# A decoder layer's expert values read in the order of a list made on the chip, with a branch around the unused ones

## The chip, the cores and the metric

The kernel runs on one core of one Trainium2 chip. The metric is the device time of one execution in microseconds. Three executions of the kernel before took 1772.38, 1773.74 and 1774.95 us; their median, 1773.74, is the time before. The profile is of one more execution, taken by the hardware profiler.

The core's engines, by the names in the profile: PE (TensorE's matmuls) and PEld (its weight loads, which overlap them), DVE (VectorE), ACT (ScalarE), POOL (GpSimd) and SP (SyncE, which here only issues transfers). Sixteen DMA engines move the data. POOL issues transfers through the queue q0, SP through q1.

## The reference

One decoder layer for 256 tokens of width 2048, float32: attention in two groups of heads, a feed-forward part called PEER, and a gated embedding, each closed by a layer norm. The change lies in PEER and in what stands around it. PEER keeps 16,384 experts, each one row of u and one row of v (2048 numbers). A token picks 16 experts in each of 8 heads, by product keys: an expert's number is 128 × ia + ib, with ia and ib out of 128 keys each.

```python
def peer_ffn(x, wq, sub_keys, u, v):
    ...
    va, ia = lax.top_k(sa, PEER_TOPK)
    vb, ib = lax.top_k(sb, PEER_TOPK)
    cand = (va[..., :, None] + vb[..., None, :]).reshape(t, PEER_HEADS, PEER_TOPK * PEER_TOPK)
    cidx = (ia[..., :, None] * PEER_NKEYS + ib[..., None, :]).reshape(t, PEER_HEADS, PEER_TOPK * PEER_TOPK)
    top, sel = lax.top_k(cand, PEER_TOPK)
    eidx = jnp.take_along_axis(cidx, sel, axis=-1)
    gates = jax.nn.softmax(top, axis=-1)
    ...
        ub = u[eb]
        vbk = v[eb]
        act = jax.nn.gelu(jnp.einsum('thed,td->the', ub, xb).astype(jnp.float32))
        w = (gb * act).astype(xb.dtype)
        return jnp.einsum('the,thed->td', w, vbk)
```

So a token's result is the sum over its 128 picks of gate × gelu(u row · x) × v row.

## The kernel before

PEER is computed in two ways at once. The first 100 of the 256 tokens (NSP) are *gathered*: for each, POOL fetches the 128 u rows that it picked by one indirect transfer of 1 MB (L890, into one of four buffers gb), VectorE takes the dot products (L857), and later the same with the v rows, which VectorE scales and accumulates (L867). The other 156 tokens (NDT) are *dense*: TensorE multiplies them with all of u and all of v, and weights that are zero where an expert wasn't picked make the sum right. GROUPS ((0,64), (64,32), (96,4)) says how the gathered tokens are laid out: in a group of n tokens, each one's 128 picks are spread over 128/n columns of partitions.

The stages, in the order of TensorE's work:

1. Attention, output projection, first layer norm, and the query projection with top-k (L206 ps_q among them). Gathers begin here.
2. u, dense: 128 blocks of 128 experts (one block for each ia; u_block, L999 to L1002). Each is one load of 1 MB by SP (wf<-peer_u) and 16 float32 matmuls of 128 × 128 by 156 columns (L206 in gemm_T32), each of which the profile shows as two instructions. ScalarE's gelu writes the block's 128 × 156 result to its place in A0 (6 blocks), A1 (up to block SEG1 = 64) or A2 (the rest); W_of gives the place.
3. Beside u's second part runs gate_work (L934 to L989) for the first 64 rows of ia, and beside v's first 64 steps for the rest. In groups of GB = 5 tokens, VectorE writes one-hot matrices of each token's picked ia (eq, L949) and ib (ohb, L951), ScalarE scales eq by the gates' high and low halves (hi, lo, L955, L956), TensorE multiplies ohb with both (L963, L964: two float16 matmuls a token and part), which gives the gate of every expert for that token, and VectorE multiplies A with it (scale, L973). OHB = 5 sets of buffers let the one-hot matrices be made ahead of the matmuls.
4. v, dense, in two passes over all 128 blocks, one for each half of the 2048 columns: v_load takes a pair of half blocks per 1 MB load by SP (wf<-peer_v), and v_mm (L1069) adds 8 matmuls of 156 columns per half block into 4 PSUM banks. v_banks (L1076) opens the banks with matmuls of zeros, v_out adds a bank into the residual XF.
5. Tail: the last STAG = 6 blocks of v are held back and multiplied column by column, so that transposes of finished columns (res1, res2), the sums of the first two gathered groups over their partitions (natural_parts, natural_out, L902 to L919) and of the third (third_sums, L921) stand between them. Then the gated embedding and the last layer norm.

What sets the order: a scheduler orders each engine's instructions when the kernel is built, and each engine then takes them in that order; instructions given to keep stay in the order of the program. Gathers are paced twice: gathers(rate) hands out so many per block (GQ 1.8 per head in the queries, GU 0.60 and GUG 0.75 per u block, GVG 0.42 and GV 0.35 per half block of v), and before each gather POOL copies a 4-byte mark that SP loads (L886 to L888), so that a gather can't run ahead of SP's loads.

## Time and profile before

| | us |
|---|---|
| median of three executions | 1773.74 (1772.38 to 1774.95) |
| the profiled execution | 1771.9 |
| its span, first to last instruction | 1770.1 |
| PE busy | 1758.6 |
| DVE busy | 1058.2 |
| ACT busy | 541.7 |
| POOL busy | 527.4 |

A row of a group reads: line, engine, operation, output<-inputs by the program's names, shapes, xcount, then busy us and mean ns of one instruction, then the engine's idle time just before them and what ended it. A matmul row gives the shape of its moving operand: 128x156 is 128 rows by 156 columns; the mean of a matmul includes the time in which the next one already runs, so the time per instruction in a dense stretch is shorter than it. A row of the chain of waits gives start, length and what it is; a row of a window gives its limits and length, then for each engine busy time and instructions, the granted clock of TensorE (1.00 is full), the busy share of the DMA engines and GB/s.

### The profile page before, as it was taken

What the parts mean: (1) busy time and instruction counts of PE and PEld (TensorE: products, weight loads), DVE (VectorE), ACT (ScalarE), POOL (GpSimd) and SP (SyncE); (2) the same over time, 40 slices, a digit from 0 to 9 for tenths busy, and PEclk for the clock granted to TensorE, in tenths of its full rate; (3) what the DMA queues carried; (4) which work ended last, traced back from release to release, by engine and by line L of the source; (5) the groups of instructions that cost most, each with busy time, mean ns of one, the idle gap of its engine ahead of it and who ended that gap; (6) DMA issues with size and microseconds to landing.
All of it is one profiled execution on the core that took longest, in us unless ns stands there. A gap on an engine that the chain in (4) does not pass through costs nothing.

```text
span 1770.1 us, 30377 instructions
## 1 busy us (share of the span) xinstructions
PE 1758.6 (99%) x12092; PEld 1650.8 (93%) x12092; DVE 1058.2 (60%) x1698; ACT 541.7 (31%) x1350; POOL 527.4 (30%) x556
## 2 busy tenths in 40 slices
PE   9999999999999999999999999999999999999998
PEld 7888888878889999999999999999999999999887
DVE  5565589664699877355655645886343433344686
ACT  5677468732110100104333324561000000000452
POOL 0133033105346227332333233323333323322000
PEclk9999999999999999999999999999999999999999
DMA  7554644566998999999999999999999999999671
GB/s 288 190 166 165 231 152 155 179 259 227 383 418 309 421 417 415 421 420 420 419 421 411 421 420 419 414 419 399 421 420 420 421 421 417 420 420 404 228 267 61
DMA packets 99823, 606.23 MB, mean 342 GB/s; under 512 B 12824, under 2 KB 14416, under 8 KB 35776
## 3 DMA queue, kind: packets, MB, share of 16 engines
q1 hardware_dynamic: 67792, 388.04, 55.3%
q0 software_dynamic: 30160, 213.10, 29.3%
q10 hardware_dynamic: 1728, 3.15, 0.5%
q8 instruction: 95, 1.56, 0.4%
q14 instruction: 48, 0.39, 0.1%
HBM read 598.36 MB, written 6.03 MB: 341 GB/s over the span
## 4 chain that ended last, share of the span: by engine, by line
PE 95%; DMA 3%; DVE 1%; issue 1%; ACT 0%; POOL 0%; POOLq 0%; ACTq 0%; SPq 0%; DVEq 0%
PE ps_v L1069 31%; PE ps_u L206 29%; PE ps_qk L194 7%; PE ps_q L206 6%; PE ps_qk L196 4%; DMA wf<-peer_u 2%; PE ps_v L213 2%; PE ps_v L215 2%; PE ps_v L214 2%; PE ps_gate L213 1%; PE ps_gate L215 1%; PE ps_gate L214 1%; PE ps_mix L214 1%; PE ps_mix L215 1%; PE ps_mix L213 1%
## 5 line engine op out<-in xcount | busy, mean ns | idle before, releaser
L1069 PE MATMUL ps_v<-A,wf 128*128 128x156 f32 x4096 | 552.4, 297 | 0.0
L1069 PEld LDWEIGHTS ps_v<-A,wf 128*128 128x128 f32 x4096 | 544.9, 190 | 0.8
L206 PE MATMUL ps_u<-XF,wf 128*128 128x156 f32 x3904 | 528.9, 297 | 1.5 <-DMA wf<-peer_u 1.2
L206 PEld LDWEIGHTS ps_u<-XF,wf 128*128 128x128 f32 x3904 | 519.2, 190 | 3.1 <-issue 1.6
L867 DVE SCALAR_TENSOR_TENSOR y<-gb,ew,y 128x2048 f32<-128x2048 f32 x94 | 220.8, 2349 | 219.1 <-DMA gb<-v_rows,eig 214.5
L857 DVE SCALAR_TENSOR_TENSOR gb<-gb,xq 128x2048 f32<-128x2048 f32 x100 | 231.7, 2322 | 146.0 <-DMA gb<-u_rows,eig 146.0
L888 POOL COPY pace<-mark 1x1 f32<-1x1 f32 x200 | 122.3, 612 | 528.6 <-DMA mark<-c_iota 527.4
L116 DVE TENSOR_TENSOR wl<-wf,wh 128x1024 fp32r<-128x1024 f32 (+1 forms) x199 | 212.7, 1091 | 103.5 <-ACT wh L115 101.6
L115 ACT CAST wh<-wf 128x1024 fp32r<-128x1024 f32 (+1 forms) x199 | 172.1, 892 | 141.8 <-PE ps_v L215 34.0
L194 PE MATMUL ps_qk<-X,wh 128*128 128x512 f32 x512 | 185.2, 401 | 0.0
L1002 ACT ACTIVATE A<-ps_u 128x156 f32<-128x156 f32 x128 | 38.4, 300 | 433.4 <-PE ps_u L206 338.2
L890 POOL DMA_INDIRECT gb<-u_rows,eig x100 | 126.6, 1266 | 125.6 <-DVE gb L857 67.6
L890 POOL DMA_INDIRECT gb<-v_rows,eig x100 | 130.0, 1300 | 65.7 <-DVE y L867 28.8
L196 PE MATMUL ps_qk<-X,wl 128*128 128x256 f32 x512 | 145.7, 285 | 0.0
L955 ACT ACTIVATE hi<-eq,ghf 128x64 f16<-128x64 f16 x312 | 104.5, 335 | 45.2 <-DVE eq L949 41.9
L194 PEld LDWEIGHTS ps_qk<-X,wh 128*128 128x128 f32 x512 | 96.4, 188 | 21.9 <-issue 1.0
L206 PE MATMUL ps_q<-XF,wf 128*128 128x256 f32 x512 | 113.6, 379 | 0.6 <-DVE XF L535 0.6
L1130 ACT COPY x<-ps_y 128x256 f32<-128x256 f32 (+3 forms) x12 | 5.2, 439 | 345.9 <-DVE st L1129 345.7
L206 PEld LDWEIGHTS ps_q<-XF,wf 128*128 128x128 f32 x512 | 95.9, 190 | 13.1 <-DVE XF L535 0.8
L956 ACT ACTIVATE lo<-eq,glf 128x64 f16<-128x64 f16 x312 | 104.2, 334 | 0.0
L196 PEld LDWEIGHTS ps_qk<-X,wl 128*128 128x128 f32 x512 | 96.3, 188 | 2.5 <-issue 1.3
L973 DVE SCALAR_TENSOR_TENSOR A<-ps_G,A 128x30 f32<-128x30 f32 (+2 forms) x96 | 32.6, 369 | 47.2 <-PE ps_G L964 34.4
(273 smaller groups left out, 1807.3 us busy)
## 6 DMA issues: line engine op xcount, KB each, us to landing
wf<-peer_v SPq DMA_DIRECT2D x128, 1024.0 KB
wf<-peer_u SPq DMA_DIRECT2D x122, 1024.0 KB
wf<-w_qk SPq DMA_DIRECT2D x64, 512.0 KB
wf<-w_out SPq DMA_DIRECT2D x32, 512.0 KB
wf<-peer_wq SPq DMA_DIRECT2D x16, 1024.0 KB
wf<-ple_gate SPq DMA_DIRECT2D x16, 1024.0 KB
wf<-w_v SPq DMA_DIRECT2D x16, 512.0 KB
wf<-w_sv SPq DMA_DIRECT2D x15, 512.0 KB
```

The lines of the kernel that those rows point to most:

```text
L115: self.order(nc.scalar.copy(wh, src))
L116: self.order(nc.vector.tensor_tensor(wl, src, wh.bitcast(F32), op=ALU.subtract))
L194: nc.tensor.matmul(ps, wh[:, j * P:(j + 1) * P], xt[:, dt, :], start=dt == 0, stop=False)
L196: nc.tensor.matmul(ps[:, :T], wl[:, j * P:(j + 1) * P], xt[:, dt, :T], start=False, stop=dt == ND - 1)
L206: nc.tensor.matmul(ps[:, :T - t0], wf[:, dt * P:(dt + 1) * P], xt[:, dt, t0:], start=dt == 0, stop=dt == ND - 1)
L857: keep(nc.vector.scalar_tensor_tensor(g, g, 1.0, xq[i], op0=ALU.mult, op1=ALU.mult, accum_out=eact[i][:, j:j + 1]))
L867: keep(nc.vector.scalar_tensor_tensor(ys[i], g, ew[i][:, j:j + 1], ys[i], op0=ALU.mult, op1=ALU.add))
L888: keep(nc.gpsimd.tensor_copy(pace, mark))
L890: keep(nc.gpsimd.indirect_dma_start(out=g, out_offset=None, in_=a[kind], in_offset=bass.IndirectOffsetOnAxis(ap=eig[i][:, 0, j:j + 1], axi ...
L955: nc.scalar.mul(hi[:, j, :], eq[:, j, :], ghf[:, t])
L956: nc.scalar.mul(lo[:, j, :], eq[:, j, :], glf[:, t])
L1069: return nc.tensor.matmul(ps[:, (j % 2) * NDT:(j % 2 + 1) * NDT], vf[:, j * P:(j + 1) * P], W_of(ia), start=False, stop=ia == NIA - 1 and ...
```

## The change

- 88 tokens are gathered, in groups of 64, 16 and 8, and 168 are dense. The last two groups are both summed by third_sums.
- gate_work runs in two parts of 68 and 60 rows of ia (SEG1 = 68), in groups of 3 tokens with 4 sets of buffers. A third matmul per token and part (ohb by eq) accumulates over all dense tokens how often each expert was picked (cnt).
- Behind each part's gates list_work makes a list. It stores the part's weights A to memory (s_w0, s_w1; 17 stores by SP in 8-row cuts), turns cnt into a mask, gives every expert a position, used ones first and the others behind them, and inverts that: for each of the 68 or 60 rows, three VectorE comparisons (row, and both planes of blk) and one matmul put each expert's number at its position. The results are idxV (rows of v) and idxW (rows of s_w).
- v runs once over all 2048 columns, in 6 PSUM banks, in blocks of 128 listed experts: v_fetch reads 128 rows of v (1 MB) and their 168 weights (86 KB) by two indirect transfers on POOL, up to LEAD = 4 blocks ahead, in 5 buffers. 46 blocks of part 0 and 40 of part 1 (CAPS) always run; the other 42 stand in a branch that is taken if the list of either part is longer than its cap (total, read into a register).
- Marks are off in v, paces are new, STAG is 3, and the sums of group 0 stand within v's second part.

```diff
-SEG1 = 64
+SEG1 = 68
-GROUPS = ((0, 64), (64, 32), (96, 4))
+PARTS = ((0, SEG1), (SEG1, SEG2))
+CAPS = (46, 40)
+GROUPS = ((0, 64), (64, 16), (80, 8))
-GU, GUG = 0.60, 0.75
-GV, GVG = 0.35, 0.42
+GU, GUG, GUL = 0.80, 0.80, 0.5
+GV, GVG = 0.7, 0.65
-GB = 5
+GB = 3
+LISTED = 6
-EARLY, HEARLY = 6, 7
-OHB = 5
-STAG = 6
+EARLY, HEARLY = 5, 7
+OHB = 4
+STAG, LEAD, NWC = 3, 4, 8
...
+                nc.tensor.matmul(cnt[:, :ns], ohb[:, j, :], eq[:, j, :], start=t0 + j == NSP,
+                                 stop=t0 + j == T - 1)
...
+        yield from list_work(oh, parts, s0, ns, cnt)
+
+    def list_work(oh, parts, s0, ns, cnt):
...
+                cuts.append((a[f"s_w{part}"][:, a0:a0 + n], At[:, c:c + n]))
...
+        keep(nc.vector.tensor_scalar(m, cnt[:, :ns], 1.0, None, op0=ALU.min))
...
+        keep(nc.tensor.matmul(ps[:ns, :P], m, ones16, start=True, stop=True))
...
+        keep(nc.tensor.matmul(ps[:, ns:ns + 1], cols[:ns], ones16[:ns, :1], start=True, stop=True))
+        keep(nc.tensor.matmul(ps[:, :ns], ahead, m, start=True, stop=False))
+        keep(nc.tensor.matmul(ps[:, :ns], cols[:ns], ahead[:ns, :ns], start=False, stop=True))
...
+        keep(nc.vector.tensor_scalar(ov, used[:, ns:ns + 1], -float(CAPS[part] * P), 0.0,
+                                     op0=ALU.add, op1=ALU.max))
...
+        for ia in range(ns):
+            row = oh.tile([P, P], F16, name="row", tag="row", bufs=2)
+            blk = oh.tile([P, 2, SEG1], F16, name="blk", tag="blk", bufs=2)
+            keep(nc.vector.tensor_scalar(row, io128, rank[:, ia:ia + 1], None, op0=ALU.is_equal))
+            keep(nc.vector.tensor_scalar(blk[:, 0, :ns], io128[:, :ns], pos[:, ia:ia + 1],
+                                         lin[:, 0:1], op0=ALU.is_equal, op1=ALU.mult))
+            keep(nc.vector.tensor_scalar(blk[:, 1, :ns], io128[:, :ns], pos[:, ia:ia + 1],
+                                         float(ia), op0=ALU.is_equal, op1=ALU.mult))
+            keep(nc.tensor.matmul(
+                ps[:, :2 * SEG1].rearrange("p (i b) -> p i b", i=2)[:, :, :ns],
+                row, blk[:, :, :ns], start=ia == 0, stop=ia == ns - 1))
+            if ia % LISTED == LISTED - 1:
+                store(1)
+                yield
...
+        keep(nc.vector.scalar_tensor_tensor(iw, ib, float(ns), pia, op0=ALU.mult, op1=ALU.add))
+        keep(nc.vector.tensor_scalar(ib, ib, float(s0 * NKEY), None, op0=ALU.add))
+        keep(nc.vector.scalar_tensor_tensor(iv, pia, float(NKEY), ib, op0=ALU.mult, op1=ALU.add))
...
+    def v_fetch(i, b, vpool, wpool, tags):
+        vf = vpool.tile([P, D], F32, name="vf", tag=tags[0], bufs=WF if vpool is sup else 2)
+        wc = wpool.tile([P, NDT], F32, name="wc", tag=tags[1], bufs=NWC if vpool is sup else 2)
+        for dst, src, idx in ((wc, a[f"s_w{i}"].rearrange("p a t -> (p a) t"), idxW[i]),
+                              (vf, a["v_rows"], idxV[i])):
+            keep(nc.gpsimd.indirect_dma_start(
+                out=dst, out_offset=None, in_=src,
+                in_offset=bass.IndirectOffsetOnAxis(ap=idx[:, b:b + 1], axis=0)))
+        return vf, wc
...
+        if ia >= NIA - 4:
+            fetched.append(v_fetch(*order.pop(0), sup, wcp, ("wf", "wc")))
+        gathers(GUG if made < 38 else GUL)
...
+    def v_blocks(n, wpool):
+        for _ in range(n):
+            while order and len(fetched) <= LEAD and (not order[0][0] or len(idxV) > 1):
+                fetched.append(v_fetch(*order.pop(0), sup, wpool, ("wf", "wc")))
+            block = fetched.pop(0)
+            for d in range(ND):
+                v_mm(d, *block, False)
...
+    for b in range(CAPS[0]):
+        if b == CAPS[0] - LEAD:
             while not done:
                 done = run(work, 1)
-        v_block(0, ia, psv)
+        v_blocks(1, wcp)
         if not done:
-            done = run(work, 1 + (ia % 8 == 7))
-        gathers(GVG if ia < SEG1 else GV)
+            done = run(work, 4 if b < 27 else 1)
+        gathers(GVG if b < 27 else GV)
+    keep(nc.vector.tensor_tensor(total, over[0], over[1], op=ALU.add))
+    more = nc.values_load(total[0:1, 0:1], min_val=0, max_val=NIA * NKEY)
+    with tc.If(more > 0):
+        for i, b in rest:
+            block = v_fetch(i, b, fbp, fbp, ("vf", "wc_"))
+            for d in range(ND):
+                v_mm(d, *block, False)
+    pools.close("fbp", "ohp", "a2p")
+    wcq = pools.open("wcq", "left", bufs=1)
+    for _ in range(LEAD + 1):
+        v_blocks(1, wcq)
         gathers(GV)
```

Lines of the changed kernel that the prediction names: L1069, L1070 and L1072 are the three comparisons of a list step, L1074 its matmul, L1083 to L1087 the last operations that make idxV and idxW, and the count and the branch follow at L1241 to L1243.

More of the change, by code (lines that the diff above doesn't have):

```diff
@@ L1038, in build @@
             A1 = a1p.tile([P, SEG1 - SEG0, NDT], F32, name="A1")
-            iaT, ibT = (a1p.tile([P, T], F16, name=nm) for nm in ("iaT", "ibT"))
-            ghf, glf = (a1p.tile([P, T], F32, name=nm) for nm in ("ghf", "glf"))
         u_block(ia, W_of(ia))
         run(work, 1)
-        gathers(GU)
+        gathers(GU if ia >= EARLY else 1.5)
     while not run(work, 1):
```

295 lines of the change are left out of this document (179 added, 116 removed).

## The prediction

> **What bounds the kernel now.** I read the profile's page first, then the two largest groups.
>
> ```profile
> PE 1758.6 (99%) x12092; PEld 1650.8 (93%) x12092; DVE 1058.2 (60%) x1698; ACT 541.7 (31%) x1350; POOL 527.4 (30%) x556
> ...
> DMA packets 99823, 606.23 MB, mean 342 GB/s; under 512 B 12824, under 2 KB 14416, under 8 KB 35776
> ...
> q1 hardware_dynamic: 67792, 388.04, 55.3%
> q0 software_dynamic: 30160, 213.10, 29.3%
> ...
> PE 95%; DMA 3%; DVE 1%; issue 1%; ACT 0%; POOL 0%; POOLq 0%; ACTq 0%; SPq 0%; DVEq 0%
> ...
> L1069 PE MATMUL ps_v<-A,wf 128*128 128x156 f32 x4096 | 552.4, 297 | 0.0
> ...
> L206 PE MATMUL ps_u<-XF,wf 128*128 128x156 f32 x3904 | 528.9, 297 | 1.5 <-DMA wf<-peer_u 1.2
> ```
>
> TensorE is busy for 99% of the span and makes 95% of the chain that ended last; nothing else is near. So a matmul removed is worth its time, and a new wait of TensorE costs its full length, since there is no idle time that could swallow it. DMA moves 342 GB/s on the mean, two thirds of it from SP's queue (q1), one third from POOL's (q0).
>
> Next the chain of waits, for what a matmul costs where TensorE never stops, and the windows of two such stretches (columns: the stretch, its length, busy time and instructions of PE, PEld, DVE, ACT, POOL, then clock, DMA share and GB/s; the third row is the first stretch again, of L206 alone).
>
> ```profile
> 514.61 6.91 PE ps_q L206 x32
> 521.96 6.91 PE ps_q L206 x32
> ...
> 1234.03 298.92 PE ps_v L1069 x2256
> ```
>
> ```profile
> 803.33:1052.87 249.54, 249.54 (x2095) 248.16 (x2095) 140.57 (x207) 88.59 (x364) 80.54 (x86) 1.00 1.01 419
> 1234.03:1532.95 298.92, 298.92 (x2258) 298.92 (x2258) 111.08 (x51) 0.00 (x0) 96.52 (x100) 1.00 1.01 420
> ```
>
> ```profile
> 803.33:1052.87 249.54, 246.42 (x1793) 238.93 (x1793) 1.00 1.01 419
> ```
>
> One v instruction of 156 columns takes 298.92/2256 = 132.5 ns. A float32 matmul is two of them, a block of 16 matmuls 4.24 us. In the first stretch 2095 − 1793 = 302 gate matmuls (L963, L964) stand among u instructions and take what those leave: (249.54 − 1793 × 0.1325)/302 = 39.6 ns each. In pure v the DMA engines are full at 420 GB/s, and yet TensorE is busy throughout: the loads run ahead there.
>
> **What TensorE gains.** All against the profiled execution, whose span is 1770.1 us.
>
> Columns 156 → 168: by proportion 142.7 ns. The two 256-column rows of the chain give 6.91/32 = 216 ns within a piece, so (216 − 132.5)/100 × 12 = 10.0 ns more, 142.5; by their starts, 7.35/32 = 230 ns, 144.2. I take 142.7 (16 matmuls: 4.57 us) and keep 144.2 as the upper end, +10 us over 6848 instructions. Then:
> - u: 128 blocks of 32 instructions, 4096 × 10.2 ns = +41.8.
> - v: 4096 × 132.5 ns = 542.7 go, 86 × 32 = 2752 at 142.7 = 392.7 come: −150.0.
> - gates: 168 tokens × 2 parts × 3 matmuls = 1008 in place of 624; 384 more at 39.6 ns = +15.2. The upper end is the busy time of the row below, 27.6 us/312 = 88 ns: +33.8.
> - the list's 128 matmuls (136 columns or fewer, float16) lie between a gate's 40 ns and a float32 half of 132 ns; nearer the gate, 60 ns: +8 (5 to 17).
> - the sums of the last groups double their 32 small matmuls, +3.7; the sums of group 0 lose 8 of 512 columns, 185.2 us/512 = 0.36 each, −2.9. Together +0.8.
>
> ```profile
> L963 PE MATMUL ps_G<-hi,ohb 128*128 128x64 f16 x312 | 27.6, 193 | 0.0
> L924 PE MATMUL ps_y<-sel,gb 128*128 128x32 f32 x32 | 3.7, 271 | 0.0
> ...
> L194 PE MATMUL ps_qk<-X,wh 128*128 128x512 f32 x512 | 185.2, 401 | 0.0
> ```
>
> Sum: 41.8 − 150.0 + 15.2 + 8 + 0.8 = **−84.2 us** of TensorE's own work.
>
> **What the list costs.** The branch's blocks are skipped only if the list shows 46 × 128 or fewer used experts in part 0 and 40 × 128 in part 1. From the inputs that the reference draws I count, over the 168 dense tokens, 5870 of 5888 and 5084 of 5120: it is not taken.
>
> The list itself is work that nothing here has done before: per row of keys three VectorE comparisons (L1069, L1070, L1072 of the changed kernel) into double buffers (row, blk), then one matmul (L1074). In the order in which the changed kernel issues its instructions most of these matmuls are spread 2 to 4 to a block, behind which VectorE's step hides. But three runs have nothing between them: 10 in part 0 some ten u blocks before v, the last 28 of part 0 with three u blocks left, and the last 36 of part 1 straight behind block 45 of v. There TensorE goes at VectorE's pace, and behind each list matmul the u or v blocks wait.
>
> One step, by the nearest rows:
>
> ```profile
> L442 DVE TENSOR_SCALAR sm<-sm,rz,nlam 128x128 f32<-128x128 f32 x8 | 3.6, 456 | 0.3
> L703 DVE TENSOR_SCALAR CJ<-CI 128x16 uint32<-128x16 uint32 x8 | 1.3, 166 | 0.1
> L703 DVE TENSOR_SCALAR CJ<-CI 128x128 uint32<-128x128 uint32 x1 | 0.2, 220 | 0.0
> ...
> L429 DVE SCALAR_TENSOR_TENSOR sm<-ps_s,dmask 128x256 f32<-128x256 f32 x16 | 6.4, 415 | 0.9 <-PE ps_s L426 0.9
> L443 DVE SCALAR_TENSOR_TENSOR sm<-sm,rz 128x256 f32<-128x256 f32 x8 | 3.8, 478 | 0.1
> ...
> L867 DVE SCALAR_TENSOR_TENSOR y<-gb,ew,y 128x2048 f32<-128x2048 f32 x94 | 220.8, 2349 | 219.1 <-DMA gb<-v_rows,eig 214.5 <-issue 4.4
> ```
>
> Without a pointer operand 16 columns take 166 ns and 128 take 220, 0.48 ns a column; a pointer adds 478 − 415 = 63 ns. So L1069 (128 columns, one pointer) is 283 ns, L1070 (68, two) 317, L1072 (68, one) 254: 0.854 us. These elements are half as wide; with half of the column term it is 0.79. I take **0.80 us**. Lower end: no pointer cost, 0.54. Upper end: the two-pointer row of 128 columns itself, 456 ns for L1070, 0.99.
>
> A run of n steps stalls TensorE for n × 0.80, plus VectorE's gather accumulations among them (2.35 us each, L867), less n × 0.06 of own work and the two steps done ahead. Ten with one accumulation: 8.0 + 2.35 − 0.6 − 1.6 = 8.2. Twenty-eight with two: 22.4 + 4.7 − 1.7 − 1.6 = 23.8. Thirty-six with none: 28.8 − 2.2 − 1.6 = 25.0. Together **57.0 us** (at 0.54: 39.3; at 0.99: 69.9).
>
> **What the end of the list costs.** Behind the last list matmul TensorE must read a register with the count and branch. VectorE first makes the indices (L1083 to L1087, four small operations, 0.8 us), then takes three accumulations that stand ahead of the count, 7.05, then the count itself, 0.2. For the register read and the branch no row exists: at least one small instruction's 0.17 us, at most the 22.5 us that a transfer is under way when the engines are full (rows below: issued 1303.37, used 1325.90, the fourth buffer on). I take 3, near the low end, because a register is four bytes and TensorE's feed pauses just then. 0.8 + 7.05 + 0.2 + 3 = **11.1 us**. Block 46's own fetch waits for the same indices: 0.8, two POOL issues of 1.3 and one 1 MB load at 420 GB/s, 2.5, about 6 to 8 us, inside the 11.
>
> ```profile
> 1303.37 0.96 POOL L890 DMA_INDIRECT gb<-v_rows,eig  x1 [0.16 <-DVE y L867]
> ```
>
> ```profile
> 1325.90 2.35 DVE L867 SCALAR_TENSOR_TENSOR y<-gb,ew,y 128x2048 f32<-128x2048 f32 x1 [5.44 <-DMA gb<-v_rows,eig]
> ```
>
> ```profile
> L890 POOL DMA_INDIRECT gb<-v_rows,eig x100 | 130.0, 1300 | 65.7 <-DVE y L867 28.8 <-issue 25.6 <-DVE eq L949 4.1
> ```
>
> **What moves between queues.** All of v now comes through POOL: two indirect transfers a block (wc 128 × 672 B, vf 1 MB), ahead of 0.65 to 0.7 gathers. In the pure part a block needs 1.049 + 0.086 + 0.65 × 1.049 = 1.816 MB in 4.57 us, 397 GB/s; the windows show 420 with both queues. POOL's own time is 2.65 × 1.3 = 3.4 of 4.57 us. So it fits, with 5% to spare. Not taking the branch makes POOL wait for its outstanding transfers, but blocks 46 to 49 are among these, 18 us of TensorE's work. I put down 4 us for the feed (0 to 37, below).
>
> SP gains 17 stores of A to memory (11 MB) that stand ahead of u loads; four blocks are loaded ahead, 18 us, and the u stage needs 413 GB/s at most (1.8 × 1.049 MB in 4.57 us): nothing, or up to the 14 us that 5.8 MB take at 420 if that lead is gone; the stall of the list then covers it. POOL loses its waits for marks in v:
>
> ```profile
> POOL pace L888 <- DMA mark<-c_iota: 527.4, 125, 10.5
> DVE y L867 <- DMA gb<-v_rows,eig: 214.5, 61, 6.1
> ```
>
> They are pacing, off the chain; VectorE has as much time without work as before.
>
> The gate stage: groups of 3 tokens, looked ahead by three groups, not of 5.
>
> ```profile
> L955 ACT ACTIVATE hi<-eq,ghf 128x64 f16<-128x64 f16 x312 | 104.5, 335 | 45.2 <-DVE eq L949 41.9 <-PE ps_G L964 3.1 <-issue 0.2
> ...
> L951 DVE TENSOR_TENSOR ohb<-io,ibT 128x640 f16<-128x640 f16 x62 | 50.7, 817 | 0.0
> ...
> L949 DVE TENSOR_TENSOR eq<-io,iaT 128x320 f16<-128x320 f16 x62 | 29.9, 483 | 6.4 <-ACT lo L956 6.4
> ...
> L973 DVE SCALAR_TENSOR_TENSOR A<-ps_G,A 128x320 f32<-128x320 f32 x31 | 15.0, 486 | 31.0 <-PE ps_G L964 18.2 <-PE ps_G L963 12.9
> ...
> L973 DVE SCALAR_TENSOR_TENSOR A<-ps_G,A 128x30 f32<-128x30 f32 x31 | 5.7, 183 | 2.5 <-PE ps_G L964 2.5
> ```
>
> With 56 groups in 38 blocks (1.47 each), VectorE pays per group some 0.36 + 0.55 + 0.49 us, times 1.47, and 0.8 accumulations of 2.35: 3.9 of 5.1 us; ACT 1.47 × 6 × 0.335 + 0.3 = 3.3. That hides, with less slack: 3 us for jitter (0 to 15).
>
> **Sum.** −84.2 + 57.0 + 11.1 + 4 + 3 = −9.1; the span becomes 1761.0. The profiled execution took 1.8 us more than its span, and the median is 1.8 above that execution: **1764.6 us**, I say 1765. The tail behind v (third sums, res1, res2, the gated part) keeps its matmuls; I count it unchanged.
>
> **Rivals.**
> (a) *The list is cheap.* If VectorE's pointers cost nothing and small float16 operations run at their floor, a step is 0.54 us: −17.7, register and branch near 0 (−3), feed and jitter hidden (−7): 1764.6 − 27.7 = **1737**. For it: no row shows this operation on float16 elements. Against it: the 456 ns row.
> (b) *POOL's queue can't feed v; slower.* Gathers and v fetches share one queue in a fixed order, and a gather that waits for VectorE or for its landing holds up the v fetch behind it. If it yields 350 GB/s, a block of the last 59 takes 1.816/350 = 5.19 us, 0.62 × 59 = 36.6, less the 4 in the sum: **1797**. It turns the sign where the feed costs 17 us, 0.29 a block, that is below 1.816/4.86 = 374 GB/s. For it: VectorE waits 214.5 us for gathers, and the 22.5 us of one transfer exceed the lead of four blocks (18.3). Against it: that delay was seen with SP's loads filling the same engines, and 420 GB/s is what these carried.
> The Trainium skill, "DMA: Bandwidth & Descriptors", section "Measured", speaks for (b): it states 341 GB/s for single 1 MB transfers issued from GpSimd and 425 for 16 MB. By the first a block would take 5.33 us, 0.76 × 59 = 45 us more and 1805 as an estimate; by the second nothing. Several transfers are outstanding here, which no row of POOL's queue alone shows.
> (c) *List and branch dear.* Steps of 0.99 us (+12.9) and a register read of 22 (+19): **1797**. The 456 ns row speaks for the first, nothing for the second.
> (d) *The branch is taken*, so the change doesn't do what it says: 42 more blocks at 4.57 us or more, +192: 1957. The counts, 18 and 36 below their limits, exclude it unless rounding moves many choices.
>
> **How the numbers follow.** Forecast 45%, with 1751 to 1779 as its own range; (a) 20%; (b) 23%; (c) 10%; (d) 2%. Within 0.2%, what a measurement can tell from no change here, is 1770.2 to 1777.3. The forecast's share splits into 0.28 faster, 0.10 same, 0.07 slower; with (a) faster is 0.48, with (b), (c), (d) slower 0.42. The range goes from 1730 ((a), with the list's matmuls at their lower end, −3, and the 256-column rows' 142.5 ns, −1, and some 3 for the tail) to 1806 (b or c, with half of the gates' upper price), which leaves out about 0.05 below and 0.12 above.
>
> **What would show it.** TensorE's idle time before L1074, 57 us, nearly all in three places; L1069, L1070 and L1072 summing to 0.80; v instructions 2752 of about 143 ns, and gaps before them named by vf or wc if (b) holds; a gap of about 11 us between the list's last matmul and block 46; busy PE down by about 84. The forecast is wrong if TensorE idles above 100 us or below 50 in the two list stages and behind them, or if v runs below 374 GB/s.

## The result, and the profile after

| | before | changed |
|---|---|---|
| median | 1773.79 us (1772.38 to 1774.95) | 1829.61 us (1828.59 to 1832.22) |
| ratio, 95% interval | | 1.0317 (1.0299 to 1.0335) |
| span of the profiled execution | 1770.1 us | 1827.2 us |
| PE busy | 1758.6 us | 1729.7 us |
| PE idle (span less busy) | 11.5 us | 97.5 us |
| mean granted clock | 0.999 | 0.969 |

The change makes the kernel 3.2% slower. The page of the changed kernel, its rows that answer to those of before:

```profile
PE 1729.7 (95%) x11288; PEld 1594.0 (87%) x11288; DVE 1097.7 (60%) x2243; ACT 554.1 (30%) x1392; POOL 618.8 (34%) x627
...
PEclk9999999999999999999999999799898969999899
...
L214 PE MATMUL ps_u<-XF,wf 128*128 128x168 f32 x3936 | 594.4, 311 | 10.6 <-DMA wf<-peer_u 10.2
...
L1199 PE MATMUL ps_v<-wc,vf 128*128 128x168 f32 x2752 | 430.8, 317 | 40.1 <-DMA vf<-v_rows,idxV 24.8
```

Two things are to be seen. PE is busy for 29 us less, not 84, and idle for 86 us more, 50.7 of them ahead of u's and v's own matmuls (last two rows). And the row PEclk, which is all nines before the change, isn't any more (1.0 is shown as 9): the granted clock falls in slices in which PE has gaps, and also in the third from the end, in which PE is busy for nine tenths or more.

What PE waited for from the start of u to block 50 of v (us in total, times, longest; PEq is TensorE's sequencer, which takes the branch at L1243):

```profile
PE ps_v L1199 <- DMA vf<-v_rows,idxV: 24.8, 9, 5.2
PE ps_list L1074 <- DVE blk L1072: 23.7, 68, 2.5
PE ps_v L1199 <- PEq L1243: 14.7, 1, 14.7
PE ps_u L214 <- DMA wf<-peer_u: 10.2, 27, 1.9
PE ps_cnt L973 <- DVE eq L957: 3.4, 2, 1.7
PE ps_cnt L973 <- DVE ohb L959: 3.0, 2, 1.6
PE ps_G L971 <- DVE A L983: 2.2, 1, 2.2
```

The list (second row) and the branch (third) are there, as forecast, but the first row is one that the sum had at a few microseconds: v's own fetches. Windows of the changed kernel by stage (length, busy time and instructions of PE, PEld, DVE, ACT, POOL, clock, DMA share, GB/s):

```profile
720.00:880.00 160.00, 156.15 (x1055) 150.26 (x1054) 73.75 (x78) 14.36 (x42) 41.70 (x66) 1.00 1.01 420
1080.00:1190.00 110.00, 91.40 (x573) 83.88 (x572) 56.77 (x222) 10.51 (x39) 20.24 (x23) 0.86 0.67 262
1282.00:1430.00 148.00, 117.78 (x920) 114.12 (x917) 71.52 (x123) 41.19 (x168) 75.25 (x61) 0.89 0.78 299
1544.40:1640.00 95.60, 95.60 (x672) 95.01 (x671) 41.28 (x31) 4.43 (x8) 74.40 (x59) 1.00 1.02 414
1680.00:1730.00 50.00, 47.49 (x285) 42.74 (x285) 23.32 (x50) 14.98 (x33) 2.32 (x3) 0.90 0.60 207
```

The first row is u, the second u beside the list, the last the small sums at the end; they are taken up below. In v's second part (fourth row) PE never stops, with the DMA engines at 414 GB/s. In the stretch of v beside gate work (third row) PE loses 30 of 148 us while the DMA engines are at 0.78. So it isn't for want of bandwidth that the fetches are late. What makes them late shows on POOL, which waited six times there, 45.2 us in all, before it could issue a gather (us in total, times, longest):

```profile
POOL gb L899 <- DVE eq L957: 45.2, 6, 11.3
```

The timeline of the changed kernel's POOL (start and length in us, line, tiles, and in brackets how long the engine stood before it and what ended that):

```profile
1364.27 0.94 POOL L1168 DMA_INDIRECT vf<-v_rows,idxV  x1 [0.30 <-issue]
1374.74 1.26 POOL L899 DMA_INDIRECT gb<-v_rows,eig  x1 [9.53 <-DVE eq L957]
1376.31 0.95 POOL L1168 DMA_INDIRECT wc<-s_w,idxW  x1 [0.30 <-issue]
```

VectorE in the same kernel and the same columns:

```profile
1371.81 0.41 DVE L983 SCALAR_TENSOR_TENSOR A<-ps_G,A 128x180 f32<-128x180 f32 x1 [2.06 <-PE ps_G L972]
1372.13 2.34 DVE L877 SCALAR_TENSOR_TENSOR y<-gb,ew,y 128x2048 f32<-128x2048 f32 x1
```

And TensorE:

```profile
1385.54 5.21 PE L1199 MATMUL ps_v<-wc,vf 128*128 128x168 f32 x18 [5.18 <-DMA vf<-v_rows,idxV]
```

Read from the end: at 1385.54 a v block starts 5.18 us late, for a fetch. One fetch of v was issued at 1364.27, the next only at 1376.31, because the gather ahead of them in POOL's order stood for 9.53 us until VectorE freed its buffer. VectorE freed it with the accumulation at 1372.13, which ended at 1374.47 (the profile names eq, the instruction behind it). In VectorE's order the accumulation stood behind the scaling of A at 1371.81, which had waited 2.06 us for TensorE's gate matmuls. And those stand in TensorE's order behind v blocks: here behind 20 instructions of v that ran at their pace, and from 1385.54 on behind a block that had waited for its own fetch. It is a ring of three queues, each of which takes its work strictly in order.

The second thing is the clock. These windows of the changed kernel (columns as above) have a run of the list in u, what stands behind it, a late fetch, and the branch:

```profile
1160.00:1170.00 10.00, 4.08 (x15) 1.56 (x15) 10.00 (x47) 0.00 (x0) 0.00 (x0) 0.50 0.27 100
1170.00:1180.00 10.00, 9.55 (x51) 9.31 (x51) 8.96 (x19) 4.77 (x20) 6.95 (x5) 0.73 0.37 127
1380.00:1390.00 10.00, 4.80 (x22) 4.71 (x23) 7.13 (x4) 0.00 (x0) 8.48 (x6) 0.51 0.72 249
1500.00:1510.00 10.00, 3.13 (x11) 3.17 (x12) 2.58 (x3) 0.00 (x0) 7.92 (x7) 0.50 0.99 365
```

The clock of TensorE is halved in 13 spells between the start of u and the tail, whose lengths are multiples of 3.41 us (6.83, 20.48, 3.41, ... in the trace's record of the clock). The spells in these windows outlast the gaps in which they began: from 1170 to 1180 PE is busy for 9.55 of 10 us, and still at 0.73. Summed over windows of 1 us from 531 to 1740, busy time times (1 − clock), the time that the half clock added to TensorE's work, is 34.5 us. Before the change it is 0. Below it is called the lost work.

### The profile page after: what moved, and what is told of

The parts are those of the page before. It is cut to its first block, busy times and chain, and to the rows that moved or that the text cites. A ratio compares the mean times of both kernels' runs of the same rounds, so it can differ in the third digit from the quotient of the medians.

```text
span 1827.2 us, 29235 instructions
## 1 busy us (share of the span) xinstructions
PE 1729.7 (95%) x11288; PEld 1594.0 (87%) x11288; DVE 1097.7 (60%) x2243; ACT 554.1 (30%) x1392; POOL 618.8 (34%) x627
## 5 line engine op out<-in xcount | busy, mean ns | idle before, releaser
L214 PE MATMUL ps_u<-XF,wf 128*128 128x168 f32 x3936 | 594.4, 311 | 10.6 <-DMA wf<-peer_u 10.2
L214 PEld LDWEIGHTS ps_u<-XF,wf 128*128 128x128 f32 x3936 | 569.6, 192 | 21.3 <-issue 15.5
L1199 PE MATMUL ps_v<-wc,vf 128*128 128x168 f32 x2752 | 430.8, 317 | 40.1 <-DMA vf<-v_rows,idxV 24.8
L1199 PEld LDWEIGHTS ps_v<-wc,vf 128*128 128x128 f32 x2752 | 412.5, 197 | 43.9 <-issue 42.7
L1102 ACT ACTIVATE A<-ps_u 128x168 f32<-128x168 f32 x128 | 39.6, 310 | 488.5 <-PE ps_u L214 476.8
L963 ACT ACTIVATE hi<-eq,ghf 128x68 f16<-128x68 f16 (+1 forms) x336 | 112.7, 335 | 132.3 <-DVE eq L957 110.9
L983 DVE SCALAR_TENSOR_TENSOR A<-ps_G,A 128x18 f32<-128x18 f32 (+2 forms) x168 | 46.8, 307 | 164.7 <-PE ps_G L972 133.1
L1168 POOL DMA_INDIRECT vf<-v_rows,idxV x86 | 111.0, 1291 | 49.3 <-issue 20.0
L1168 POOL DMA_INDIRECT wc<-s_w,idxW x86 | 95.9, 1116 | 83.0 <-DVE ib L1086 34.2
L964 ACT ACTIVATE lo<-eq,glf 128x68 f16<-128x68 f16 (+1 forms) x336 | 112.1, 334 | 0.0
L214 PEld LDWEIGHTS ps_q<-XF,wf 128*128 128x128 f32 x512 | 95.8, 190 | 12.4
```

What stands on the lines that cost most here:

```text
L214: nc.tensor.matmul(ps[:, :T - t0], wf[:, dt * P:(dt + 1) * P], xt[:, dt, t0:], start=dt == 0, stop=dt == ND - 1)
L963: nc.scalar.mul(hi[:, j, :], eq[:, j, :], ghf[:, t])
L964: nc.scalar.mul(lo[:, j, :], eq[:, j, :], glf[:, t])
L1168: keep(nc.gpsimd.indirect_dma_start(out=dst, out_offset=None, in_=src, in_offset=bass.IndirectOffsetOnAxis(ap=idx[:, b:b + 1], axis=0)))
L1199: return nc.tensor.matmul(psv[d // 3][:, d % 3 * NDT:(d % 3 + 1) * NDT], vf[:, d * P:(d + 1) * P], wc, start=False, stop=last and (d % 3 = ...
```

## The experiments

All ratios are to the kernel before, run beside them; the changed kernel itself stands at 1.0317.

### The accumulations of gathers left out of v's first part

```diff
...
-                keep(nc.vector.scalar_tensor_tensor(ys[i], g, ew[i][:, j:j + 1], ys[i],
-                                                    op0=ALU.mult, op1=ALU.add))
+                if marked or i > 0 or done2[0]:
+                    keep(nc.vector.scalar_tensor_tensor(ys[i], g, ew[i][:, j:j + 1], ys[i],
+                                                        op0=ALU.mult, op1=ALU.add))
```

From the start of v to block 46 `done2[0]` is false, so that no gather of group 0 is added up there.

> Between the start of v and block 46 the gathers are fetched as before, byte for byte, but VectorE doesn't accumulate them (group 0's part of the result is left incomplete). Theory 1 (order): v's fetches come late because on POOL's queue they stand behind a gather whose buffer VectorE frees only between pieces of gate work, which in turn wait for TensorE; then the stretch of v with gate work loses most of its 44 us of excess, and the time is 1775 to 1795 us. Theory 2 (bytes): v and gathers ask for more than the queue carries; the bytes are the same, so 1822 to 1832. Theory 3 (gate work alone is too much for VectorE and ScalarE): some 16 us of waits for one-hot tiles remain, 1810 to 1820.

Measured: 1781.4 us (one execution), 48 us less. The same window as the third row above, in this kernel:

```profile
1282.00:1430.00 148.00, 145.02 (x1216) 141.38 (x1215) 48.45 (x176) 41.19 (x163) 64.31 (x66) 1.00 0.91 353
```

And what its POOL waited for (us in total, times, longest):

```profile
POOL vf L1170 <- PE ps_v L1201: 72.0, 38, 3.0
```

PE is busy for 145 of 148 us (118 before), at full clock, and there is no wait for a fetch between 1190 and 1430 any more, although more bytes go through (353 GB/s, not 299). POOL now waits for TensorE to free v's buffers, 72 us in all: the fetches run as far ahead as five buffers allow. Theory 1 holds, bytes are out, and of the rest of the gate work little remains: PE waits 3.0 us in this stretch, for list steps. The edit takes work from VectorE too, but time was not what it lacked: in the changed kernel it was busy for 71.5 of the 148 us.

### Gathers given out ahead of the gate work, and accumulated one gather earlier

```diff
         v_blocks(1, wcp)
+        gathers(GVG if b < 27 else GV)
         if not done:
             done = run(work, 4 if b < 27 else 1)
-        gathers(GVG if b < 27 else GV)
```

> In v's first part a block's gathers, with their accumulation on VectorE, are given out ahead of the block's gate work and not behind it. Theory 1 (order): the accumulation frees the buffer sooner, v's fetches come earlier: 1800 to 1820 us. Theory 2 (bytes): no change, 1826 to 1833.

Measured: 1819.4 us, 1.0258 (1.0237 to 1.0280). Ten microseconds go; the waits for fetches between 1190 and 1430 us fall from 21.0 to 12.3 us, the ring is looser but not open. With the second half of it, four gathers under way made three:

```diff
-                    while len(made) >= NGB - (kind == "v_rows" and i == 2):
+                    while len(made) >= NGB - (not marked or (kind == "v_rows" and i == 2)):
```

> As the run in which gathers go ahead of the gate work, and in v each gathered buffer is also accumulated one gather earlier (three, not four, under way), so that the next gather finds its buffer free when POOL comes to it; in v's first part the list also keeps its pace of before. Theory 1 (order on POOL's queue): the waits of v for its fetches between 1300 and 1430 us go, 1785 to 1805. If VectorE now waits for landings and the gate work gets late instead: 1815 to 1835.

Measured: 1814.2 us, 1.0245 (1.0226 to 1.0263), between the two expectations, and not clear of the run before it, whose interval it overlaps. The gate work runs freely up to 1379 us (2.0 us of waits for fetches from 1282 on), and then one wait of 12.4 us and, at the branch, one of 22.4 stand where several small ones stood.

### The list given out twice as fast in v's first part

```diff
-            done = run(work, 4 if b < 27 else 1)
+            done = run(work, 4 if b < 27 else 2)
```

> In v's first part the list's work is given out twice per block from block 27 on, not once, so that the list of part 1 is complete nearly three blocks of v ahead of the branch, and no run of 36 list matmuls stands ahead of it. If the list's end is what the branch waits for, the run (18 us) and the wait at the branch (14.7 us) both go and the clock stays up there: 1795 to 1808 us. If the branch costs its own 14.7 us wherever it stands: 1808 to 1816. If the early runs cost as much as the late one: 1822 to 1830.

Measured: 1839.7 us, 1.0374 (1.0343 to 1.0404): slower, against all three expectations. The list does end earlier and the run ahead of the branch is gone. But its POOL, in the timeline:

```profile
1462.31 0.94 POOL L899 DMA_INDIRECT gb<-v_rows,eig  x1 [25.66 <-DVE row L1069]
...
1487.51 2.93 POOL L899 DMA_INDIRECT gb<-v_rows,eig  x1 [13.07 <-DVE y L877]
```

One gather stood for 25.66 us until VectorE came past its list steps, a later one for 13.07, and v's fetches behind them: PE waited 12.8 us for one of them, up to 1500.26, shortly ahead of the branch. So a list step isn't only dear where TensorE waits for it. With two places for row and blk, VectorE can be two steps ahead of TensorE and no more; whatever stands behind a list step on VectorE, the accumulations of gathers among it, waits for TensorE too. That is the ring once more, closed by the list.

### The branch left out

```diff
-    more = nc.values_load(total[0:1, 0:1], min_val=0, max_val=NIA * NKEY)
-    with tc.If(more > 0):
-        for i, b in rest:
-            block = v_fetch(i, b, fbp, fbp, ("vf", "wc_"))
...
```

> The branch with its 42 blocks, the count and the reading of it are left out; the 86 blocks run as before, which is right for these inputs. Block 46's fetch still waits for the list. If the wait at the branch (14.7 us) is the price of reading the register and of what stands ahead of the count: about 8 us of it stay as wait for block 46's weights, 1816 to 1824 us. If it is only the fetch that shows there: 1827 to 1831.

Measured: 1823.6 us, 1.0270 (1.0241 to 1.0299): 6 us less, and 8.9 us of wait for block 46's fetch remain where 14.7 stood, as the first theory had it. What the branch costs can be seen in the changed kernel, by line (duration in ns least, median and most; first and last start):

```profile
L1243 PEldq COMPARE_BRANCH  x1: 5681/5681/5681, 1500.9 to 1500.9; - x1
```

The branch takes 5.68 us on TensorE's sequencer and 45 to 76 ns on those of the other four engines; reading the register takes TensorE 0.49 us. In the twelve kernels here that have the branch, it takes TensorE's sequencer 3.7 to 6.5 us. Why it is so long on TensorE alone is not shown; the skipped blocks hold 42 × 32 of TensorE's matmul instructions, and no run varied their number.

### The sums of the last two groups, spread

```diff
+        if b >= N1 - STAG - 4:
+            q = 4 * (b - N1 + STAG + 4)
+            third_sums(ps3, q, q + 4)
...
-            third_sums(ps3, 0, ND)
```

> The 64 small matmuls (32 columns) of the last gathered groups' sums, which stand in one piece of 9.3 us within a spell of 10.24 us at half clock although TensorE is never idle in it, are spread in four pieces between v's blocks 33 to 36. Nothing is removed. Theory C (the clock is cut after a few us of little work in TensorE, whether it waits or multiplies small tiles): the spell goes, and the time falls by 4 to 6 us, to 1822 to 1827. If the spell has nothing to do with these matmuls: 1828 to 1832.

Measured: 1829.0 us, 1.0314 (1.0300 to 1.0329). This run tells nothing of the theory, since the small matmuls still ran in one piece, from 1688.2 to 1697.6. But it shows the clock at work in a place without any gap. TensorE in the timeline of this kernel (each row two matmuls; the pace is from start to start):

```profile
1688.35 0.39 PE L931 MATMUL ps_y<-sel,y 128*128 128x32 f32 x2
1688.57 0.39 PE L931 MATMUL ps_y<-sel,gb 128*128 128x32 f32 x2
...
1692.93 0.61 PE L931 MATMUL ps_y<-sel,gb 128*128 128x32 f32 x2
1693.36 0.61 PE L931 MATMUL ps_y<-sel,y 128*128 128x32 f32 x2
```

Two matmuls of 32 columns take 0.22 us at first, and 0.43 from 1692.5 on, with no idle time between them. The second attempt:

```diff
...
             for i, block in enumerate(held):
                 keep(v_mm(d, *block, i == STAG - 1))
+            if d < 6:
+                third_sums(ps3, (0, 3, 6, 9, 12, 14)[d], (3, 6, 9, 12, 14, 16)[d])
```

> Once more the changed kernel with its 64 small matmuls spread; the spread before didn't come about, as these matmuls had to wait for their last gathers and still ran in one piece. Here they stand in six pieces between the held v matmuls of the first two banks, and nothing else is moved but the addition of their sums by one bank. Theory C (the clock is cut after a few us of little work in TensorE, idle or with small tiles): the spell of 10.24 us at half clock in the tail goes, 1822 to 1827 us. Otherwise 1828 to 1832.

Measured: 1824.8 us, 1.0298 (1.0281 to 1.0315): 4.9 us less with the same instructions. The window of the small sums in this kernel:

```profile
1680.00:1730.00 50.00, 47.52 (x312) 42.14 (x311) 27.98 (x55) 18.74 (x39) 1.20 (x3) 1.00 0.67 237
```

312 matmuls where 285 stood in the same 50 us, and the clock at 1.00, not 0.90. The windows of 1 us give 5.0 us of lost work in this stretch of the changed kernel, where the 64 small matmuls stood between v matmuls with no idle time before or among them, and 0 here. The Trainium skill, "TensorE: Matmul & The Clock Gate", section "What's actually happening", states that TensorE's clock is halved after an idle window of about 3.4 us, counted by a free-running monitor, and full again after a busy one. The trace agrees in the factor, 0.5, and in the length, 3.41 us and its multiples; what it has beyond that is a spell behind a stretch in which PE is shown as busy throughout, with nothing but small matmuls.

### Three steps of the list at a time

This is the run with gathers ahead and accumulated earlier, with the first spread of the small sums, and:

```diff
-LISTED = 6
+LISTED = 3
...
-            done = run(work, 4 if b < 27 else 1)
+            done = run(work, 4 if b < 27 else 2)
```

> The run before it together with the spread small matmuls, and the list given out in pieces of three steps, two pieces per block of v, so that accumulations of gathers stand between them. If the list's second part loses its long run and gathers no longer wait behind list steps, the run before it is beaten by 15 to 30 us: 1765 to 1785. If list steps again hold the gathers, and these v's fetches: 1800 to 1825.

Measured: 1800.1 us, 1.0156 (1.0141 to 1.0172): 14 us less than the run with gathers ahead and accumulated earlier, and at the low end of the second expectation. PE still waited 21.3 us at the branch, where VectorE took three accumulations, one of them 6.4 us late, ahead of the count.

### Everything eased but the list's two places

```diff
-        if made < 38:
-            run(work, 3)
+        if made < 29:
+            run(work, 4)
         elif ia < NIA - 5:
-            run(work, 1)
+            run(work, 2)
...
-            done = run(work, 4 if b < 27 else 1)
+            done = run(work, 5 if b < 23 else 2)
...
+        if b == 36:
...
+            keep(nc.vector.tensor_tensor(total, over[0], over[1], op=ALU.add))
+            more = nc.values_load(total[0:1, 0:1], min_val=0, max_val=NIA * NKEY)
```

with gathers ahead and accumulated earlier, lists in threes, small sums spread.

> All four causes are eased together: gathers' buffers freed one gather earlier; the gate work of both parts given out faster so that the lists end several blocks before they are needed; list steps in pieces of three; the count read eight blocks of v ahead of the branch; small matmuls spread. If the waits found so far are the whole of it, idle time of TensorE in v falls below 25 us, the half-clock spells behind the stalls go with it, and the time is 1735 to 1765, below the kernel before. If the bytes of gathers and v fetches together are the limit after all, or VectorE with the faster gate work: 1775 to 1800.

Measured: 1839.1 us, 1.0370 (1.0352 to 1.0387): worse than the changed kernel, and outside both expectations. POOL in the timeline of this kernel:

```profile
1485.32 2.62 POOL L1168 DMA_INDIRECT wc<-s_w,idxW  x1 [18.18 <-issue]
```

And POOL's own reading of the count, by line:

```profile
L1242 POOLq TENSOR_LOAD <-total x1: 504/504/504, 1484.1 to 1484.1; - x1
```

A fetch of v is issued 18 us after the gather ahead of it, and PE waits 16.2 us for it. The row says issue, that is, the fetch itself waited for nothing that the profile shows. What stood between is the reading of the count. POOL takes it in its order as the other engines do, it now stands ahead of that fetch, and the count was made only at 1483.87, behind the last list step and an accumulation. So this wait belongs to the early reading, which this run added. PE also stood for 6.9 and 7.4 us ahead of v's opening matmuls, where the changed kernel has no wait; what held it there was not traced. And a gather had waited 13 us for VectorE at 1458.63, as in the run with the list twice as fast. The run altered too much at once to price these apart. What had not been touched so far was what holds the list steps: two places.

### Twelve places for the list's tiles

```diff
-            row = oh.tile([P, P], F16, name="row", tag="row", bufs=2)
-            blk = oh.tile([P, 2, SEG1], F16, name="blk", tag="blk", bufs=2)
+            if ia % 3 == 0:
+                row3 = oh.tile([P, GB, P], F16, name="row", tag="ohb", bufs=OHB)
+            row = row3[:, ia % 3, :]
+            blk = oh.tile([P, GB * ns], F16, name="blk", tag=("eq", "hi", "lo")[ia % 3], bufs=OHB)
+            blk = blk[:, :2 * ns].rearrange("p (i b) -> p i b", i=2)
...
```

> The changed kernel with one thing altered: the list's tiles row and blk take turns in twelve places (those of the one-hot tiles, free by then) and not in two, so that VectorE can run up to twelve steps ahead of TensorE, and the long runs of list matmuls break up. If the runs are costly only because VectorE is held two steps ahead of TensorE, and gathers stand behind held list steps: 10 to 14 us of idle time and some half-clock time go in u, 20 to 25 us at the end of part 1, 1785 to 1805. If VectorE's work in the lists is what is too much, no change: 1822 to 1832.

Measured: 1785.8 us, 1.0079 (1.0049 to 1.0108): 44 us less by this alone. What PE waited for in this kernel, the first and third row (us in total, times, longest; the second, 13.3 us, is u's loads):

```profile
PE ps_v L1202 <- DMA vf<-v_rows,idxV: 22.6, 11, 4.1
PE ps_v L1202 <- PEq L1246: 9.0, 1, 9.0
```

And its window of u beside the list:

```profile
1080.00:1190.00 110.00, 103.04 (x751) 98.28 (x750) 64.53 (x240) 16.78 (x65) 31.84 (x33) 0.98 0.85 337
```

Of PE's waits for list steps 0.2 us are left (23.7 before); between 1080 and 1190 us, 751 matmuls are done where the changed kernel did 573. The branch costs 9.0 us, not 14.7. In idle time and lost work together some 20 us go there and 18 us between 1430 and 1545, at the end of the second list. The waits for v's fetches remain, 22.6 us where 24.8 stood.

### All of it together

```diff
...
-            done = run(work, 4 if b < 27 else 1)
+            done = run(work, 4 if b < 27 else 3)
+        if b == 40:
...
+            keep(nc.vector.tensor_tensor(total, over[0], over[1], op=ALU.add))
+            more = nc.values_load(total[0:1, 0:1], min_val=0, max_val=NIA * NKEY)
```

with the twelve places, gathers ahead and accumulated earlier, lists in threes (twice per u block behind the gate work), small sums spread.

> The twelve places for the list's tiles, the accumulation one gather earlier, gathers ahead of gate work, list in pieces of three steps at twice the pace, the count read six blocks of v ahead of the branch, small matmuls spread. If gathers held by VectorE, list runs and the branch are all of it: 1735 to 1770. If the ring of queues (v waits for POOL, POOL for VectorE, VectorE for TensorE) stays shut by the gate work alone: 1775 to 1800.

Measured: 1761.4 us, 0.9928 (0.9905 to 0.9950): faster than the kernel before, by 0.7%. Its page:

```profile
PE 1707.4 (97%) x11288; PEld 1578.3 (89%) x11288; DVE 1096.2 (62%) x2243; ACT 555.4 (31%) x1392; POOL 625.2 (35%) x627
```

And what its PE waited for, the longest rows among them:

```profile
PE ps_u L214 <- DMA wf<-peer_u: 10.3, 24, 4.1
PE ps_list L1077 <- DVE blk L1075: 6.7, 19, 1.7
PE ps_list L1077 <- DVE row L1072: 6.1, 3, 5.1
PE ps_v L1202 <- remote: 5.5, 1, 5.5
PE ps_v L1202 <- DMA vf<-v_rows,idxV: 3.1, 1, 3.1
```

The waits for v's fetches are down to 3.1 us, and the lost work to 12.3 us by the same windows of 1 us; the waits for u's loads are what they were. The list still costs 12.8 us of waits. The wait called remote is the one at the branch: the count was made at 1427.66, TensorE read it at 1441.3 in 0.49 us, and the branch then took its sequencer 6.45 us; v goes on at 1449.54. An early count takes away the wait for it, not the branch's own time. PE is busy for 22 us less than in the changed kernel, with the same 11288 matmuls. From 531 to 1740 us idle time is 42 us less than in the changed kernel and lost work 22 us less, 64 together; the span is shorter by 63.4. So these two account for the gain.

### Fewer gathers beside u

```diff
-GU, GUG, GUL = 0.80, 0.80, 0.5
-GV, GVG = 0.7, 0.65
+GU, GUG, GUL = 0.72, 0.80, 0.5
+GV, GVG = 0.70, 0.83
```

on top of the run before.

> The run before it (twelve places for the list's tiles and the rest) with fewer gathers beside u's first part (0.72 per block, not 0.80) and as many more beside v's first part (0.83, not 0.65). Between 720 and 880 us u's matmuls went at 152 ns where 142 is their pace, with the DMA engines at 420 GB/s. If that is a limit of bytes, some 8 us of it go and v's first part, at 300 to 340 GB/s, has room: 1750 to 1757. If v's first part pays for it with gathers that hold up v's fetches: 1758 to 1775.

Measured: 1761.2 us (1756.4 to 1777.0), 0.9937 (0.9915 to 0.9958): the same. The stretch of u between 720 and 880 us kept its pace: 1040 u instructions and 69 gate matmuls in 160 us, with some 3 us for the gates 151 ns per u instruction. But the run didn't take the bytes off, either: the DMA engines were as full as before, at 420 GB/s, with 28 gathers issued in the stretch where the run before had 33. So whether bytes set u's 152 ns there, where 142 were forecast, stays open.

## Why the prediction was wrong

The forecast was 1765 us, faster than before, with a range from 1730 to 1806; measured were 1829.6, slower. Step by step:

**TensorE's own work, −84.2: right, but for some 5 us.** 2752 instructions of v were run, not 4096 (the page's last row above): the branch was not taken. The gates came at 42 to 47 ns, not 39.6, which makes the 5 us. In v's second part, 320 instructions in the chain of waits (start, length, line, count) take 142.5 ns each; the forecast was 142.7:

```profile
1575.95 45.60 PE ps_v L1199 x320
```

**"A new wait of TensorE costs its full length": this failed.** It costs more. 86 us of idle time came, near the 75 forecast, but 34.5 us of work at half clock came with it, and that is why PE busy fell by 29 us only. The run with the small sums spread takes the 5.0 us of its stretch out by their order alone; that the others go back to gaps is read from where the spells stand, and from their shrinking as gaps go (to 22 us without the accumulations, 12 in the best run). It isn't in proportion: over the experiments the lost work is 0.27 to 0.55 of the idle time. In the kernel before the clock was full from u to the tail, so its profile had no row for this; the prediction had no term for it and no rival.

**The feed, "4 us (0 to 37)", and the jitter of the gates, "3 us (0 to 15)": the mechanism was named, its place and size were wrong.** The waits for v's fetches and for the gates came to 24.8 + 3.4 + 3.0 + 2.2 = 33 us of idle time, and 12.5 us of the lost work stand in the same stretch (1282 to 1430). Rival (b) had said that a gather waiting for VectorE holds up the v fetch behind it, which is the mechanism that was found, and then priced it as bandwidth spread over the last 59 blocks. The waits for fetches stand elsewhere: 6.7 us ahead of blocks 17 to 26, 14.3 ahead of blocks 31 to 37, with the queues at 299 GB/s in this stretch, beside or just behind the gate work, where VectorE, POOL and TensorE wait for each other in turn. Block 50 waited 3.7 us, which goes back to another step: that POOL waits at the branch for its outstanding transfers was foreseen and held to be covered by blocks 46 to 49, but POOL stood for 10.4 us, up to 1521.36, and block 50's fetch came late. The blocks behind it ran without a wait up to the tail, with the engines full, though (b) had priced them too. Also, by the forecast's own sum its sign turns where the feed costs 13 us (9.1 above the 4), not 17, which is where the result would be slower beyond the 0.2%. Besides, the prediction took the two paces in v the wrong way round: 0.70, not 0.65, stands in the last blocks, so they needed 409 GB/s, not 397. They got it from POOL's queue alone (packets, MB, and share of the engines' time, in the window from 1544.4 to 1640):

```profile
q0 software_dynamic: 6282, 39.49, 101.1%
```

39.49 MB in 95.6 us is 413 GB/s. Of the two figures that the page "DMA: Bandwidth & Descriptors" of the Trainium skill offered (section "Measured"), 425 GB/s for large transfers and 341 for single ones of 1 MB, several outstanding transfers of 1 MB are near the first.

**The list, 57.0: too dear by 20.** The three long runs took 4.6, 18.6 and 18.2 us (10, 28 and 36 steps), 41.4 in all; less their own 4.4, 37 us. The prices of the instructions were right, and yet a step wasn't their sum. The groups of VectorE (busy, mean ns of one | idle before):

```profile
L1069 DVE TENSOR_SCALAR row<-io,rank 128x128 f16<-128x128 f16 x128 | 32.8, 256 | 67.6 <-PE ps_list L1074 65.0 <-issue 2.3
L1070 DVE TENSOR_SCALAR blk<-io,pos,lin 128x68 f16<-128x68 f16 x68 | 20.1, 295 | 0.0
L1072 DVE TENSOR_SCALAR blk<-io,pos 128x68 f16<-128x68 f16 x68 | 15.9, 235 | 0.0
```

and its timeline in a run of the list:

```profile
1484.04 0.25 DVE L1069 TENSOR_SCALAR row<-io,rank 128x128 f16<-128x128 f16 x1
1484.20 0.29 DVE L1070 TENSOR_SCALAR blk<-io,pos,lin 128x60 f16<-128x60 f16 x1
1484.41 0.23 DVE L1072 TENSOR_SCALAR blk<-io,pos 128x60 f16<-128x60 f16 x1
1484.55 0.25 DVE L1069 TENSOR_SCALAR row<-io,rank 128x128 f16<-128x128 f16 x1
```

256 + 295 + 235 = 786 ns, where 800 was forecast. But the next one starts 0.16 to 0.21 us after the one before, while that still runs, and a step comes every 0.51 us. Rival (a)'s 0.54 us was right on this point by luck: it had left the pointers' cost out, while the durations have it and overlap. But the runs are not all that the list cost. The sum took the two places as given and left out that a held list step holds the accumulations behind it; with twelve places 44 us went.

**The end of the list, 11.1: 14.7.** The three accumulations took 7.1 us as forecast. The register read and the branch took 6.6 us (count done at 1500.23, PE at work at 1506.87), not 3. The forecast priced the reading, which took 0.49 us; the 5.68 us of the branch itself had no price of their own. VectorE and then PE in the timeline:

```profile
1493.05 7.11 DVE L877 SCALAR_TENSOR_TENSOR y<-gb,ew,y 128x2048 f32<-128x2048 f32 x3
1500.08 0.15 DVE L1241 TENSOR_TENSOR total<-ov,ov 128x1 int32<-128x1 f32 x1
```

```profile
1506.87 5.44 PE L1199 MATMUL ps_v<-wc,vf 128*128 128x168 f32 x26 [14.72 <-PEq L1243]
```

**u and SP's queue, "nothing": 10.2 us of waits for u loads**, and u's matmuls at 152 ns between 720 and 880 us, about 6 us beyond those waits. The forecast's 413 GB/s stood 2% below what the engines carry, and it was called free. It had 0.8 gathers to a u block, but in that window 32 were issued beside 33 u loads, so that more was asked for than 413; the engines were full at 420.

Sum of the terms as measured: 37 + 14.7 + 33 + 10.2 + 34.5, less 7 of lost work that lies inside the list's runs (1151 to 1172 and 1473 to 1493) and is counted in the 37, is 122 us against the 75.1 of the forecast. With 5 for the gates and 6 for u that is 58 us more than forecast, on −9.1: +49 of the +57.1 that the spans show. Some 8 us were not traced to a place. The two largest errors are the clock (27.5 us outside the list's runs, where nothing was forecast) and the feed with the gates (33 where 7 were forecast); sign and range both failed on them.

## What to carry to other kernels

Where three engines take their work in fixed orders and feed each other, look for the ring: a transfer that waits for a buffer holds every transfer behind it on its queue, so what frees that buffer must not itself stand behind something that waits for the transfers' user. Two places between a producer and a consumer tie the producer's whole queue to the consumer; here twelve places instead of two were worth 44 us, and giving out the list twice as fast without them cost 10. A value read by every engine stands in every engine's order, so reading it ahead of the work that makes it holds up engines that don't need it yet (POOL, for 18 us, in the run that eased everything else). And price a stall of TensorE with the half-clock spell that it may bring: in a kernel whose TensorE was hardly ever idle, 86 us more of idle time came with 29.5 us of lost work (34.5 less the 5.0 of the small sums).

## What the runs showed of the hardware

- TensorE's clock halves not only behind gaps. 64 matmuls of 32 columns, back to back and with PE shown as busy, brought a spell of 10.24 us at half clock; their pace went from 0.22 to 0.43 us per pair 4 to 5 us into the piece.
- VectorE's instructions overlap as the profile counts them: three of 256, 295 and 235 ns start within 0.51 us. Their durations can't be added up to a pace; starts in a dense row of them can.
- A register read and a branch on it cost 6.6 us of TensorE, from the end of the VectorE instruction that made the value to the first matmul behind it. The branch alone is 5.68 of it on TensorE's sequencer (3.7 to 6.5 in the twelve kernels with it) and 45 to 76 ns on the other engines; having the value earlier didn't shorten it.
- POOL's queue alone moved 413 GB/s, nearly as much as both queues together before the change (420).
